# Reciprocal roots of the norms from GpSimd to VectorE, in a hybrid decoder step with expert gathers

## The chip, the cores and the metric

The kernel runs on one core of a Trainium2 chip. The metric is the device time of one execution in microseconds (us). TensorE is called PE (its weight loads PEld), VectorE DVE, ScalarE ACT, GpSimd POOL and SyncE SP.

## The reference, cut to what matters

One layer of a decoder is computed for a prompt of 1024 tokens and for a group of 64 sample tokens (8 sequences of 8), with the same weights.

- `n = RMSNorm(x)`; a wide projection `n @ w_in` feeds three branches: GLA (gated linear attention, with an RMSNorm per head of its output), FoX (softmax attention with forget gates, paged cache for the sample group) and attention over 256 memory tokens, whose keys and values come from `RMSNorm(mem) @ w_mem_kv`.
- `h = x + W_out(sum of gated branches)`.
- `h = h + PEER(RMSNorm(h))`: each token has 8 heads; each head takes the top 16 of 128x128 experts by two lists of keys, and the token's output is a sum over its 128 chosen experts of `gelu(x . u_e) * gate * v_e`.
- `y = RMSNorm(h)`.

`RMSNorm` is `x * rsqrt(mean(x*x) + 1e-6) * g`. All of it is float32. The reciprocal root of one number per row (or two, for the two heads of a GLA half) is all that the change touches in the arithmetic.

## The kernel before, in words

The 1024 prompt tokens are eight blocks (0 to 7) of 128 rows, the sample group is block 8 with 64 rows. `base(grp)` takes three blocks through everything up to the PEER's scores; it runs for `[0, 1, 2]`, `[3, 4, 5]` and `[8, 6, 7]`. In `base` the order of the code is: `norm_T` for the three blocks (load, square sum on ACT, reciprocal root, scaling on DVE, transposes on PE); per half the projections by `mm_w` (raw weights by SP, a rounded high part `wh` on ACT, the rest `wl` on DVE at L267, three matmuls on PE) with `gla` and `fox_prompt` between them; memory attention; the merge; `w_out`; a norm of `h` (`rstd_of`, scaling at L900, transposes at L314); the projection by `w_pq` with the keys' scores (L915) and `top16`.

After that a block goes one of two ways. Blocks 0, 1, 2, 6 and 7 are gathered: `choose(b)` finds the 128 experts of each token, and `peer_gather(b)` fetches, slot by slot, the rows of `peer_u` (L1065) and `peer_v` (L1076) with indirect DMAs that GpSimd issues; DVE multiplies and sums each `u` row tile (L1067) and adds each weighted `v` row tile to `acc` (L1082). The row tiles are four in number (five at the end), so GpSimd's next gather waits until DVE is through with an older row. Blocks 3, 4, 5 and 8 are dense: `expert_weights(b)` spreads the gates over all experts with PE, ACT and DVE, and `peer_dense` multiplies with all 16384 experts on PE at the end. `finish` adds `h`, takes the last norm (L1043 to L1047) and stores a block.

The order of each engine's instructions is written before the run by the framework, from its own estimates and from priorities: `at` gives `choose` and `expert_weights` the most urgent one, `base` the ordinary one by its place in the code, and `gather` a later one, so gathers fill in beside `base` of the next group. Each engine then goes through its own list in order.

The reciprocal roots stand at three places, all on GpSimd: `rstd_of` (called by `norm_T` and for the norm of `h`; L305 and L306), `gla` (L473 and L474, used at L478) and `finish` (L1045 and L1046, used at L1047). Each is two instructions on a tile of one or two columns:

```python
G.tensor_scalar(r, ss, scale, EPS, op0=OP.mult, op1=OP.add)
G.tensor_tensor(r, r, neghalf[:, :n], op=OP.pow)
```

In `gla` the PSUM tile `po`, one of two of the tag `g` that nearly all transposes use, is held until L478 has read it.

Of the kernel before, what the change touches and what calls it, by code (L numbers as in the profile page):

```python
# [18 lines left out]
F32 = mybir.dt.float32  # L19
F32R = mybir.dt.float32r  # L20
BF = mybir.dt.bfloat16
I32 = mybir.dt.int32
# [3 lines left out]
OP = mybir.AluOpType  # L26
AX = mybir.AxisListType

D = 1024
EPS = 1e-6  # L30
# [13 lines left out]
DENSE = [3, 4, 5, SAMPLE]  # L44
# [10 lines left out]
def tile_hybrid(ctx: ExitStack, tc: tile.TileContext, x_prompt, x_sample, cache_fox_k, cache_fox_v,  # L55
# [23 lines left out]
    def T(tag, shape, dt=F32):  # L79
        cnt[0] += 1  # L80
        return bp.tile(shape, dt, tag=tag, name=f"{tag}_{cnt[0]}", bufs=BUFS[tag])

    def const(shape, dt=F32, pool=ec):
        cnt[0] += 1
        return pool.tile(shape, dt, name=f"c{cnt[0]}", tag=f"c{cnt[0]}")
# [128 lines left out]
    pgt = const([64, 1], I32)  # L214
    SP.dma_start(pgt, page_table.rearrange("b (p o) -> (b p) o", o=1))

    neghalf = const([128, 8], F32, cp)
    G.memset(neghalf, -0.5)

    def rows(ap, n, p=128):  # L220

        return bass.AP(tensor=ap.tensor, offset=ap.offset, ap=[[0, p], [1, n]])
# [78 lines left out]

    def rstd_of(ss, n, scale):

        r = T("sm", [128, n])
        G.tensor_scalar(r, ss, scale, EPS, op0=OP.mult, op1=OP.add)  # L305
        G.tensor_tensor(r, r, neghalf[:, :n], op=OP.pow)  # L306
        return r

    def split_T(src_cols, hi, lo, k0):

# [8 lines left out]
    def norm_T(src, nrows, gain, hi, lo):  # L319

        x = T("wr", [128, 1024])
        if nrows < 128:
            G.memset(x, 0.0)
        SP.dma_start(x[:nrows], src)
        ss = T("sm", [128, 1])
        junk = T("P", [128, 1024], BF)
        A.activation(junk, x, AF.Square, accum_out=ss)
        r = rstd_of(ss, 1, 1.0 / D)
        V.scalar_tensor_tensor(x, x, r, gain, op0=OP.mult, op1=OP.mult)
        for k0 in (0, 4):  # L330
            split_T([x[:, (k0 + i) * 128:(k0 + i + 1) * 128] for i in range(4)], hi, lo, k0)
# [57 lines left out]
    def gla(blk, half, qT, zk, zv, zr, glrT, oT):  # L389
        smp = blk == SAMPLE  # L390
        P = 64 if smp else 128
# [77 lines left out]
        junk = T("X", [128, 2, 128])  # L469
        for i in range(2):  # L470
            A.activation(junk[:P, i], po[:P, i * 128:(i + 1) * 128], AF.Square, accum_out=ss[:P, i:i + 1])
        r = T("sm", [128, 2])
        G.tensor_scalar(r[:P], ss[:P], 1.0 / 128, EPS, op0=OP.mult, op1=OP.add)  # L473
        G.tensor_tensor(r[:P], r[:P], neghalf[:P, :2], op=OP.pow)  # L474
        og = T("X", [128, 256])
        for i in range(2):
            sl = slice(i * 128, (i + 1) * 128)
# [160 lines left out]
    def base(grp):  # L638
# [72 lines left out]
        for half in range(2):  # L711
# [9 lines left out]
            if half == 0:  # L721
                px = proj_small()
                glrT = T("sm2", [17, NT])
                G.memset(glrT, 1.0)
                for b in grp:
                    c = T("sm", [128, 16])
                    V.tensor_copy(c, px[b][:, :16])
                    pt = PS("f")
                    PE.transpose(pt[:16, :wid[b]], c[:wid[b]], ident[:wid[b], :wid[b]])
                    evac(glrT[:16, off[b]:off[b] + wid[b]], pt[:16, :wid[b]])  # L730
                    if b == SAMPLE:
                        lfs[0] = logf_sample(px[b][:64, 16:24])
                    else:
                        logf_prompt(b, px[b][:, 16:24])
# [141 lines left out]
        for c in range(4):  # L876
            pz, _ = halves(grp)
            mm_w(w_out[0], 8, c * 256, jobs_of(grp, pz, mT))
            hc = T("z", [128, len(grp), 256])
            for i, b in enumerate(grp):  # L880
                src, n = xsrc(b)
                xc = T("ge", [128, 256])
                if n < 128:
                    G.memset(xc, 0.0)
                SP.dma_start(xc[:n], src[:, c * 256:(c + 1) * 256])
                p = pz[b]
                ht = hc[:, i]
                V.tensor_tensor(ht, p[:, :256], xc, op=OP.add)  # L888
                A.activation(xc, ht, AF.Square, accum_out=ss[b][:, c:c + 1])
                SP.dma_start(h_scr[b][:, c * 256:(c + 1) * 256], ht)  # L890
                h[b].append(ht)
# [146 lines left out]
    def finish(b, y, ht, gfin):  # L1038

        P = 64 if b == SAMPLE else 128  # L1040
        V.tensor_tensor(y[:P], y[:P], ht[:P], op=OP.add)
        s1 = gp.tile([128, 1], F32, tag="fs" if b not in DENSE else "fsd", name=f"fs{b}", bufs=2)
        A.activation(ht[:P], y[:P], AF.Square, accum_out=s1[:P])  # L1043
        r = gp.tile([128, 1], F32, tag="fr" if b not in DENSE else "frd", name=f"fr{b}", bufs=2)
        G.tensor_scalar(r[:P], s1[:P], 1.0 / D, EPS, op0=OP.mult, op1=OP.add)  # L1045
        G.tensor_tensor(r[:P], r[:P], neghalf[:P, :1], op=OP.pow)  # L1046
        V.scalar_tensor_tensor(y[:P], y[:P], r[:P], gfin[:P], op0=OP.mult, op1=OP.mult)  # L1047
        if b == SAMPLE:
            SP.dma_start(y_sample.rearrange("b t d -> (b t) d"), y[:P])
        else:  # L1050
            SP.dma_start(y_prompt[0, b * 128:(b + 1) * 128, :], y)
# [213 lines left out]
    def fox_sample(lfn, oT, fill):  # L1265
# [8 lines left out]
        lf = T("P", [128, 8, 8, 8])  # L1274
        A.activation(lf.rearrange("s b p h -> s h (b p)"), p.rearrange("s (h n) -> s h n", h=8), AF.Copy)
        pre = T("wr", [128, 8, 9, 8])
        G.memset(pre[:, :, 0, :], 0.0)
        for pg in range(8):
            V.tensor_tensor(pre[:, :, pg + 1, :], pre[:, :, pg, :], lf[:, :, pg, :], op=OP.add)
        ndp = []  # L1280
# [12 lines left out]
        evac(ndn, p[:8, :64])  # L1293

        Qz = T("kv", [128, 4, 8, 64])
        G.memset(Qz, 0.0)
        kn = T("zq", [128, 4, 64])
        vn = T("P", [64, 512])
        SP.dma_start(vn, fox_v_sample[0].rearrange("b t h d -> (b t) (h d)"))
# [88 lines left out]

    def mem_sample(qs, oT):
        Qz = T("kv", [128, 4, 8, 32])  # L1390
        G.memset(Qz, 0.0)
        for hh in range(4):
            V.tensor_copy(Qz[:, hh, :, hh * 8:hh * 8 + 8],
                          qs[hh // 2][:, hh % 2, :64].rearrange("p (b t) -> p b t", t=8))
# [126 lines left out]
```

## Time and profile before

| | |
|---|---|
| median of 3 runs | 4340.33 us (4328.08 to 4341.13) |
| profiled execution, its own time | 4325.89 us |
| its span | 4324.1 us |
| busy share of the span | PE 86%, PEld 75%, DVE 77%, ACT 42%, POOL 39% |
| mean granted clock of TensorE | 0.909 of full speed |
| gathers | 640 rows of `u`, 640 of `v` |
| reciprocal roots on POOL | 47 (20 by `rstd_of`, 18 in `gla`, 9 in `finish`) |

Read the span as three stretches. Up to about 650 us `base` of the first group runs without gathers. From there to about 2830 us `base` of the second and third groups share the engines with the gathers of blocks 0, 1 and 2, `choose` and `expert_weights`. From there to the end the dense part runs on PE beside the gathers of blocks 6 and 7.

### The profile page before, as it was taken

The numbers are of one execution on the slowest core, as the hardware profiler recorded it, in microseconds if no ns is written. First come the engines' busy times: TensorE is split into PE (matmuls) and PEld (weight loads), VectorE is DVE, ScalarE is ACT, GpSimd is POOL, SyncE is SP. The second block draws the span as 40 slices with busy tenths as digits, with TensorE's granted clock in tenths as the row PEclk, the third lists the DMA queues.
The fourth block names the chain that finished last, engine by engine and source line by source line (L and its number), as shares of the span: only waits on it lengthen the run. The fifth ranks groups of instructions, "written<-read, shape, count | busy, mean of one in ns | idle before, by whom it ended". The sixth has DMA issues, their size and how long they took to land. (4 is left out here: it accounts for less than half of the span.)

```text
span 4324.1 us, 62414 instructions
## 1 busy us (share of the span) xinstructions
PE 3719.4 (86%) x21306; PEld 3260.5 (75%) x21306; DVE 3338.8 (77%) x7924; ACT 1821.1 (42%) x3710; POOL 1691.6 (39%) x1466
## 2 busy tenths in 40 slices
PE   4999898779777876887888976867999999999997
PEld 4989797768656774776665656756998899889997
DVE  3444479988779898988865458988998888788883
ACT  2565544345444324665664434353332233223322
POOL 0000003554454445446454544414444445454440
PEclk9999998889778976896889998988999999999999
DMA  3334457989889977888888899968989999899992
GB/s 112 109 101 142 138 166 246 307 259 324 282 307 322 307 250 250 285 271 285 286 275 297 282 342 341 321 214 311 310 303 330 338 335 332 315 330 340 342 310 83
DMA packets 665781, 1168.08 MB, mean 270 GB/s; under 512 B 63309, under 2 KB 453093, under 8 KB 661878
## 3 DMA queue, kind: packets, MB, share of 16 engines
q0 software_dynamic: 193616, 704.99, 46.7%
q1 hardware_dynamic: 471846, 459.09, 32.7%
q8 instruction: 169, 2.77, 0.2%
q14 instruction: 150, 1.23, 0.1%
HBM read 1086.82 MB, written 77.11 MB: 269 GB/s over the span
## 5 line engine op out<-in xcount | busy, mean ns | idle before, releaser
L1065 POOL DMA_INDIRECT u<-in_peer_u_dram,ei x640 | 787.2, 1230 | 863.4 <-DVE a L1067 391.2
L1076 POOL DMA_INDIRECT v<-in_peer_v_dram,ei x640 | 764.8, 1195 | 871.5 <-DVE acc L1082 411.7
L1082 DVE SCALAR_TENSOR_TENSOR acc<-v,a,acc 128x1024 f32<-128x1024 f32 x635 | 812.7, 1280 | 68.5 <-DMA v<-in_peer_v_dram,ei 65.5
L1067 DVE CUSTOM_DVE_ANT_0 u<-u,x 128x1024 f32<-128x1024 f32 x640 | 774.4, 1221 | 76.8 <-DMA u<-in_peer_u_dram,ei 76.2
L265 ACT ACTIVATE wh<-wr 128x512 fp32r<-128x512 f32 x568 | 354.3, 630 | 551.8 <-PE pj L274 175.5
L267 DVE TENSOR_TENSOR wl<-wr,wh 128x512 fp32r<-128x512 f32 x568 | 388.7, 688 | 156.7 <-PE pj L277 54.1
L1235 PE MATMUL py<-dwh,dvh 128*128 128x448 f32 x1024 | 375.4, 370 | 35.1 <-ACT dwh L1222 31.0
L1212 PE MATMUL pa<-xh,duh 128*128 128x448 f32 x1024 | 384.5, 375 | 3.9 <-ACT duh L1193 3.9
L273 PE MATMUL pj<-aT,wh 128*128 128x384 f32 (+1 forms) x1104 | 373.6, 344 | 12.1 <-ACT tq L99 7.3
L1213 PE MATMUL pa<-xl,duh 128*128 128x448 f32 x1024 | 380.2, 371 | 0.0
L1236 PE MATMUL py<-dwl,dvh 128*128 128x448 f32 x1024 | 376.0, 368 | 1.5 <-DVE dwl L1223 1.5
L1237 PE MATMUL py<-dwh,dvl 128*128 128x448 f32 x1024 | 374.1, 368 | 2.0 <-DVE dvl L1231 2.0
L274 PE MATMUL pj<-aT,wh 128*128 128x384 f32 (+1 forms) x1104 | 367.9, 337 | 1.5 <-DVE aT L317 1.5
L1230 ACT ACTIVATE dvh<-dvr 128x1024 fp32r<-128x1024 f32 x128 | 134.0, 1058 | 394.1 <-PE py L1236 191.8
L281 PE MATMUL pj<-wh,aT 128*128 128x256 f32 x944 | 263.4, 303 | 36.0 <-DVE z L888 8.8
L282 PE MATMUL pj<-wh,aT 128*128 128x256 f32 x944 | 261.4, 299 | 6.6 <-DVE aT L872 5.3
L277 PE MATMUL pj<-aT,wl 128*128 128x384 f32 (+1 forms) x1104 | 261.6, 341 | 5.8 <-DVE wl L267 5.8
L1215 PE MATMUL pa<-xh,dul 128*128 128x448 f32 x1024 | 239.4, 369 | 0.0
L1235 PEld LDWEIGHTS py<-dwh,dvh 128*128 128x128 f32 x1024 | 192.5, 189 | 52.2 <-ACT dwh L1222 31.2
L273 PEld LDWEIGHTS pj<-aT,wh 128*128 128x128 f32 x1104 | 217.2, 197 | 19.2 <-ACT tq L99 11.4
L281 PEld LDWEIGHTS pj<-wh,aT 128*128 128x128 f32 x944 | 193.4, 206 | 43.0 <-DVE z L739 8.2
L274 PEld LDWEIGHTS pj<-aT,wh 128*128 128x128 f32 x1104 | 217.6, 197 | 2.8 <-DVE aT L317 2.4
(489 smaller groups left out, 8328.5 us busy)
## 6 DMA issues: line engine op xcount, KB each, us to landing
wr<-in_w_in_dram SPq DMA_DIRECT2D x168, 512.0 KB, 5.1
dvr<-in_peer_v_dram SPq DMA_DIRECT2D x128, 512.0 KB, 7.1
dur<-in_peer_u_dram SPq DMA_DIRECT2D x128, 512.0 KB, 6.3
dc<-c_scr SPq DMA_DIRECT2D x15, 1792.0 KB, 16.7
wr<-in_w_pq_dram SPq DMA_DIRECT2D x48, 512.0 KB, 5.7
c_scr<-stg SPq DMA_DIRECT2D x24, 1024.0 KB, 6.3
wr<-in_w_out_dram SPq DMA_DIRECT2D x24, 512.0 KB, 6.4
u<-in_peer_u_dram,ei POOLq DMA_INDIRECT x640, 6.3
```

Source lines behind the costliest of these rows:

```text
L267: V.tensor_tensor(wl, raw[:, q2:q2 + 2], wh.bitcast(F32), op=OP.subtract)
L273: PE.matmul(ps, wh[:, i, c], hi[:, k], start=k == 0, stop=False)
L274: PE.matmul(ps, wh[:, i, c], lo[:, k], start=False, stop=False)
L281: PE.matmul(ps, hi[:, k, :], wh[:, i], start=k == 0 and first, stop=False)
L1065: G.indirect_dma_start(out=r, out_offset=None, in_=UR, in_offset=bass.IndirectOffsetOnAxis(ap=ei[:, s:s + 1], axis=0))
L1067: V.tensor_tensor_reduce(r, r, x2, 1.0, 0.0, OP.mult, OP.add, a[:, s:s + 1])
L1076: G.indirect_dma_start(out=r, out_offset=None, in_=VR, in_offset=bass.IndirectOffsetOnAxis(ap=ei[:, s:s + 1], axis=0))
L1082: V.scalar_tensor_tensor(acc, r, a[:, s:s + 1], acc, op0=OP.mult, op1=OP.add)
L1212: PE.matmul(pa[:, :NT], uh[:, k], xh[:, k], start=k == 0, stop=False)
L1213: PE.matmul(pa[:, :NT], uh[:, k], xl[:, k], start=False, stop=False)
L1235: PE.matmul(py[:, :NT], vh[:, j], wh, start=j == 0, stop=False)
L1236: PE.matmul(py[:, :NT], vh[:, j], wl, start=False, stop=False)
```

## The change: what it does

All 47 reciprocal roots go to VectorE. `rsqrt` makes thirteen instructions of each pair: the scaled sum `x`; its bits as an integer turned into a float, `-0.5 * bits + 1597463007`, turned back into an integer and read as a float, which is a guess `y`; and three Newton steps of three instructions each. Each of the thirteen reads what the one before it wrote. `rstd_of` and `gla` now take three tiles of the tag `sm` (12 buffers) instead of one. The memsets inside the groups (in `norm_T`, `glrT`, the residual's tile, `pre` and the two `Qz`) also go to VectorE; `neghalf` disappears. The memsets of the set-up stay on GpSimd.

```diff
-    neghalf = const([128, 8], F32, cp)
-    G.memset(neghalf, -0.5)
...
     def rstd_of(ss, n, scale):
-        r = T("sm", [128, n])
-        G.tensor_scalar(r, ss, scale, EPS, op0=OP.mult, op1=OP.add)
-        G.tensor_tensor(r, r, neghalf[:, :n], op=OP.pow)
-        return r
+        return rsqrt(ss, scale, [T("sm", [128, n]) for _ in range(3)])
+
+    def rsqrt(ss, scale, tmp):
+        x, y, t = tmp
+        V.tensor_scalar(x, ss, scale, EPS, op0=OP.mult, op1=OP.add)
+        V.tensor_copy(t, x.bitcast(I32))
+        V.tensor_scalar(t, t, -0.5, 1597463007.0, op0=OP.mult, op1=OP.add)
+        V.tensor_copy(y.bitcast(I32), t)
+        for _ in range(3):
+            V.scalar_tensor_tensor(t, y, -0.5, y, op0=OP.mult, op1=OP.mult)
+            V.tensor_tensor(t, t, x, op=OP.mult)
+            V.scalar_tensor_tensor(y, t, 1.5, y, op0=OP.add, op1=OP.mult)
+        return y
...
-            G.memset(x, 0.0)
+            V.memset(x, 0.0)
...
-        r = T("sm", [128, 2])
-        G.tensor_scalar(r[:P], ss[:P], 1.0 / 128, EPS, op0=OP.mult, op1=OP.add)
-        G.tensor_tensor(r[:P], r[:P], neghalf[:P, :2], op=OP.pow)
+        r = rsqrt(ss[:P], 1.0 / 128, [T("sm", [128, 2])[:P] for _ in range(3)])
...
-                G.memset(glrT, 1.0)
+                V.memset(glrT, 1.0)
...
-                    G.memset(xc, 0.0)
+                    V.memset(xc, 0.0)
...
-        r = gp.tile([128, 1], F32, tag="fr" if b not in DENSE else "frd", name=f"fr{b}", bufs=2)
-        G.tensor_scalar(r[:P], s1[:P], 1.0 / D, EPS, op0=OP.mult, op1=OP.add)
-        G.tensor_tensor(r[:P], r[:P], neghalf[:P, :1], op=OP.pow)
+        r = gp.tile([128, 3], F32, tag="fr" if b not in DENSE else "frd", name=f"fr{b}", bufs=2)
+        r = rsqrt(s1[:P], 1.0 / D, [r[:P, i:i + 1] for i in range(3)])
...
-        G.memset(pre[:, :, 0, :], 0.0)
+        V.memset(pre[:, :, 0, :], 0.0)
...
-        G.memset(Qz, 0.0)
+        V.memset(Qz, 0.0)
```

## Rows read from the trace of the kernel before

**Rows 1.** Windows: us; per engine busy us (instructions); granted clock, DMA share, GB/s

```profile
83.00:657.00 574.00, 541.94 (x3593) 504.89 (x3592) 287.63 (x833) 309.95 (x659) 13.51 (x26) 0.96 0.44 132
657.00:1513.00 856.00, 682.60 (x3879) 595.70 (x3879) 737.73 (x1901) 366.42 (x754) 418.10 (x360) 0.84 0.88 296
1513.00:2830.00 1317.00, 1055.39 (x6286) 845.37 (x6286) 1034.45 (x2723) 644.93 (x1455) 634.17 (x535) 0.85 0.85 289
2830.00:4310.00 1480.00, 1409.52 (x7355) 1286.81 (x7355) 1241.84 (x2332) 476.94 (x803) 618.29 (x520) 0.98 0.88 304
```

**Rows 2.** Groups of instructions by line, POOL, 657 to 1513 us

```profile
L1065 POOL DMA_INDIRECT u<-in_peer_u_dram,ei x176 | 216.4, 1229 | 227.0 <-DVE a L1067 89.5 <-DVE acc L1082 32.4 <-DVE tp L933 17.9
L1076 POOL DMA_INDIRECT v<-in_peer_v_dram,ei x156 | 181.3, 1162 | 193.3 <-DVE acc L1082 71.1 <-DMA v<-in_peer_v_dram,ei 15.8 <-DVE a L1067 15.6
```

**Rows 3.** Groups of instructions by line, POOL, whole span

```profile
L474 POOL TENSOR_TENSOR sm<-sm,c 128x2 f32<-128x2 f32 (+1 forms) x18 | 18.3, 1018 | 1.4
L306 POOL TENSOR_TENSOR sm<-sm,c 128x1 f32<-128x1 f32 x20 | 11.6, 585 | 1.4
...
L1046 POOL TENSOR_TENSOR fr<-fr,c 128x1 f32<-128x1 f32 (+1 forms) x9 | 6.3, 699 | 0.6
```

**Rows 4.** Timeline: one reciprocal root of `norm_T` in the first stretch

```profile
50.48 0.19 ACT L327 ACTIVATION_READ_ACCUMULATOR P<-wr 128x1 f32 x1
...
51.64 1.28 DVE L329 SCALAR_TENSOR_TENSOR wr<-wr,sm,kv 128x1024 f32<-128x1024 f32 x1 [0.67 <-POOL sm L306]
```

**Rows 5.** Timeline of DVE, first stretch: L547 needs L545; L727 needs neither

```profile
112.43 0.17 DVE L545 SCALAR_TENSOR_TENSOR sm<-sm,sm 128x8 f32<-128x8 f32 x1
112.63 0.17 DVE L547 TENSOR_TENSOR sm<-sm,sm 128x8 f32<-128x8 f32 x1
112.72 0.17 DVE L727 COPY sm<-f 128x16 f32<-128x16 f32 x1
```

**Rows 6.** Timeline of DVE, second stretch: the same pair, first and last of six

```profile
718.25 0.15 DVE L545 SCALAR_TENSOR_TENSOR sm<-sm,sm 128x8 f32<-128x8 f32 x1
...
722.80 0.24 DVE L547 TENSOR_TENSOR sm<-sm,sm 128x8 f32<-128x8 f32 x1
...
1643.49 0.15 DVE L545 SCALAR_TENSOR_TENSOR sm<-sm,sm 128x8 f32<-128x8 f32 x1
...
1647.69 0.15 DVE L547 TENSOR_TENSOR sm<-sm,sm 128x8 f32<-128x8 f32 x1
```

**Rows 7.** Groups by line, whole span: the `v` half of the gathers' DVE work

```profile
L1082 DVE SCALAR_TENSOR_TENSOR acc<-v,a,acc 128x1024 f32<-128x1024 f32 x635 | 812.7, 1280 | 68.5 <-DMA v<-in_peer_v_dram,ei 65.5
```

**Rows 8.** Timeline: `gla`'s root in the second stretch, first and last of twelve

```profile
809.51 0.20 ACT L471 ACTIVATION_READ_ACCUMULATOR X<-g 128x1 f32 x1
...
815.56 0.60 DVE L478 SCALAR_TENSOR_TENSOR X<-g,sm,z 128x128 f32<-128x128 f32 x2
...
2115.92 0.20 ACT L471 ACTIVATION_READ_ACCUMULATOR X<-g 128x1 f32 x1
...
2120.48 0.61 DVE L478 SCALAR_TENSOR_TENSOR X<-g,sm,z 128x128 f32<-128x128 f32 x2 [1.52 <-POOL sm L474]
```

**Rows 9.** Timeline of PE: first transposes after the norm of `h`, second group

```profile
1425.27 1.12 PE L314 MATMUL g<-c,z 128*128 128x128 f32 x4 [4.29 <-DVE z L900]
```

**Rows 10.** Waits of PE, 657 to 2820 us: us in total, times, longest

```profile
PE g L481 <- DVE X L478: 9.8, 4, 4.6
```

**Rows 11.** Waits of POOL, 657 to 2820 us: us in total, times, longest

```profile
POOL sm L305 <- ACT P L327: 16.9, 5, 5.2
POOL fr L1045 <- ACT h L1043: 3.4, 1, 3.4
```

**Rows 12.** Windows: a slice with many gathers, columns as in the first group

```profile
2376.00:2484.00 108.00, 102.42 (x708) 75.23 (x707) 55.36 (x109) 53.60 (x116) 61.15 (x54) 0.98 0.83 285
```

**Rows 13.** Timeline of DVE: last step of block 7, and of the last block

```profile
4210.28 1.28 DVE L1047 SCALAR_TENSOR_TENSOR acc<-acc,fr,gf 128x1024 f32<-128x1024 f32 x1 [0.74 <-POOL fr L1046]
...
4317.39 1.28 DVE L1047 SCALAR_TENSOR_TENSOR dvr<-dvr,fr,dur 64x1024 f32<-64x1024 f32 x1 [0.97 <-POOL fr L1046]
```

More of the change, by code (lines that the diff above doesn't have):

```diff
@@ L1390, in mem_sample @@
         Qz = T("kv", [128, 4, 8, 32])
-        G.memset(Qz, 0.0)
+        V.memset(Qz, 0.0)
         for hh in range(4):
```

## The prediction, as put on record before the run

> **What bounds the kernel now.** I first cut the span into stretches with the windows view [rows 1]. In the first group (83 to 657 us) PE is busy 542 of 574 us, DVE only half of the time, and there are no gathers. In the dense part (2830 to 4310) PE is busy 1410 of 1480 us at a granted clock of 0.98, so PE sets the length there. Between them nothing is full: DVE is busy 738 of 856 us in the second group and 1034 of 1317 in the third, PE about 80% at a clock near 0.85. The second group has the same prompt work as the first and takes 856 us where that took 574, and the difference is what gathers and `choose` add: 282 us beside 332 gathers [rows 2], 0.85 us a gather. So in the mixed stretch `base` and the gathers lengthen each other although no engine is full.
>
> How they do it shows in the timeline of DVE. A step that needs the step before it starts 0.20 us after it in the first stretch; one that needs nothing follows after 0.09 us [rows 5]. In the mixed stretch the same dependent step starts 4.55 us later in the first pass and 4.20 us in the last of the six [rows 6]: gather sums of 1.28 us [rows 7], `wl` subtractions and top-16 work have been written in between. A chain of small dependent steps on DVE is cheap in busy time there and dear in latency. The change makes 47 such chains (18 in `gla`, 20 in `rstd_of`, 9 in `finish`) [rows 3] of 13 steps.
>
> **The change, part by part.**
>
> *First stretch.* The root on GpSimd now costs 0.97 us from the end of ACT's sum to DVE's use (50.48 + 0.19 to 51.64) [rows 4]. Thirteen dependent steps at 0.20 are 2.6 us, so +1.6 where it stands alone; three blocks interleaved are 39 instructions at 0.09, 3.5 us, +2.5. Three places stand before work that PE has to wait for (memory norms, first norms, the norm of `h`): 7.5 us. Six roots in `gla` at 1.6 are 9.6 if PE has nothing else and 0 if it has; I take half. Sum +12 (between 0 and 17). Here a page speaks: the Trainium skill, "VectorE: DVE Perf Modes", section "The DRAIN you can't avoid", says that a chain of DVE operations takes the same time with a semaphore after each as with one after the last. By it a dependent step would also cost 0.09 us, a lone chain 1.2 us, and this term would be about 8; the trace does not agree (0.20 against 0.09, rows 5), and the row is taken.
>
> *Mixed stretch, latency.* In `gla` a root now takes 5.9 us from ACT's sum to DVE's use at its first pass and 4.4 at its last [rows 8]; I take 5. The new chain's step is bounded by 0.20 us below [rows 5] and by 4.5 above [rows 6]. I take 2.0: where `base` stands still, `wl` work is missing, so a step hosts about one gather sum (1.28) and some top-16 work. 13 x 2.0 = 26, so +21 us per chain. Where does it stand on `base`'s path? At the norm of `h` of both groups PE has nothing else of `base` to do: already now it stands idle 4.29 us there [rows 9]: 2 x 21 = 42. At both groups' first norms the tail of the `w_pq` projection covers some: 2 x 12 = 24. In `gla` (12 times) the next projection covers most; PE waited for L478 four times in this stretch [rows 10], which would make 4/12 x 21 = 7 each, and the order is written knowing the chain: 3 each, 36 (between 0 and 84). Sum 102. But gathers run on while `base` stands: in a slice where they run well GpSimd issues 54 in 108 us, 0.50 a us [rows 12]. 102 us hold 51 gathers, which `base` need not share with later, 0.85 us each: 43 back. Net +59.
>
> *Mixed stretch, GpSimd set free.* GpSimd's queue is in order: a root that waits for ACT parks the gathers behind it. It waited 16.9 + 3.4 = 20 us so between 657 and 2820 [rows 11]; at 332 gathers in 856 us these are 8 gathers, 8 x 0.85 = 7: -7. Nothing larger is to be had: the rest of GpSimd's idle time is waiting for DVE to free a row [rows 2].
>
> *Memsets.* Ten pieces of some 5,900 columns in all; the trace shows no memset on DVE. Bounds: 0 (hidden in its idle time) to 7 us (at the 1.28 us that a sum over 1024 columns takes [rows 7]). +3, between the ends, since some stand in front of a load and some do not.
>
> *Dense part and end.* `finish` of blocks 6 and 7 gets longer, while two row tiles and `acc` are held. Cover: block 7's last step starts at 4210, the end is at 4317 [rows 13], so some 100 us are free: 0. If that cover were gone, 2 x 21 us would be paid. The very last root costs 0.97 us of DVE's wait [rows 13] and becomes 2.6: +2 with the one before it.
>
> Sum: 12 + 59 - 7 + 3 + 2 = +69 us. The profiled execution took 4325.9 us, 14 less than the median of the three runs, so 4395 us; against that median it is +1.3%.
>
> **Rivals.** *A, faster.* The order keeps each chain's steps together (0.20 us, 2.6 us in all), which beats today's 5 us in the mixed stretch. Then the four places there give 4 x 2.4 = 10, `gla` a third of 12 x 2.4, 10, the parked gathers 7, against 6 (half of the first stretch's 12) and 2 at the end: -19, about 4307 us. It decides if a step takes under 5/13 = 0.4 us in the mixed stretch. For it: chains of three blocks can fill each other's gaps. Against it: [rows 6].
>
> *B, DVE's time is all it costs.* The latencies are covered by gathers and projections, and what is left is 27 chains x 13 = 351 instructions at 0.09 us, 32 us, in a stretch where DVE is busy 82% (1772 of 2173 us, rows 1): 26. With +12, -7 and +2 that is +33, 4359 us. The Trainium skill's "Perfetto Trace Analysis", section "Optimizing Scalar/DVE Operations", stands beside this: it advises to take work off a saturated DVE, even to GpSimd, and the change goes the other way. The trace agrees that DVE is the fuller of the two there.
>
> *C, the full latency.* Steps of 3.6 us (47 us, +42 per chain), `gla` a third exposed: 2 x 42 + 2 x 33 + 12 x 14 = 318, 135 given back by gathers: +183 in place of +59, 4519 us. For it: [rows 6], and that `po` holds one of two PSUM tiles `g` through the chain. Against it: gathers that finish early leave DVE to `base`.
>
> **Chances.** The forecast (4355 to 4440) 0.48; B (4335 to 4375) 0.20; C (over 4440) 0.15; A (4290 to 4327) 0.17. About 0.3%, 13 us, is what a measurement of this kernel can tell from no change. From the median 4340 that puts A in faster, 0.17; of B and the forecast's low edge 0.12 within; the rest, 0.71, slower. The likeliest case's own range is 4355 to 4440; the range that holds it 8 times in 10 must reach into A and C: 4310 to 4480, leaving out about 0.1 on each side.
>
> **What would show it.** Right: in the mixed stretch the steps of `rsqrt` start 1.3 to 4 us apart, with L1067, L1082 and L267 between them; PE's wait at the transposes after the norm of `h` grows from 4 to over 15 us; the second and third groups get longer, the dense part (about 1480 us) does not; the first stretch ends some 10 us later. Wrong: steps of 0.2 us everywhere (A); PE's waits at L314 unchanged and only DVE's share up (B). A dense part longer by more than 10 us would say that the end of the gathers has become the bound, which I exclude. The whole order is written anew with the change, so places that it does not touch can move by some us either way.

## The result, and the profile after

The changed kernel takes 4513.2 us (median of 4 runs, 4509.3 to 4517.5) where the kernel before took 4340.7 beside it: a ratio of 1.0417, 95% interval 1.0392 to 1.0442 (the two medians alone give 1.0398). The change makes the kernel slower, as forecast, but by 173 us where 54 were forecast; 4513 lies outside the range (4310 to 4480). Between the two profiled executions it is 183 us against a sum of 69. It is almost the number of rival C, 4519, though not by rival C's terms (below).

First the page's busy times (share of the span, instructions), kernel after:

```profile
span 4507.5 us, 62907 instructions
...
PE 3766.7 (84%) x21306; PEld 3293.6 (73%) x21306; DVE 3408.9 (76%) x8546; ACT 1824.7 (40%) x3710; POOL 1600.4 (36%) x1360
```

Before, the page gave PE 3719.4, DVE 3338.8 and POOL 1691.6 us in a span of 4324.1. The span grows by 183 us, PE's busy time by 47 and DVE's by 70: 136 us of the growth is time in which PE stands still. PE runs the same 21306 matmuls; they took longer, with a mean granted clock of 0.884 where it was 0.909. So the 622 instructions more on DVE are not the bill by themselves; somebody waits for them.

The windows view of the kernel after, cut at the same events as [rows 1] (scaling of the first norms at the start of the first, second and third group, dense part, end):

```profile
87.00:703.00 616.00, 566.58 (x3639) 522.63 (x3637) 330.29 (x1149) 316.65 (x673) 5.72 (x6) 0.92 0.43 129
703.00:1674.00 971.00, 684.38 (x3891) 597.69 (x3891) 825.35 (x2193) 369.25 (x759) 467.25 (x388) 0.81 0.87 291
1674.00:2994.00 1320.00, 1065.12 (x6206) 852.11 (x6206) 962.03 (x2646) 638.35 (x1434) 507.28 (x441) 0.83 0.78 263
2994.00:4494.00 1500.00, 1422.23 (x7361) 1294.57 (x7362) 1246.37 (x2350) 476.87 (x800) 617.20 (x512) 0.97 0.89 299
```

The first window is 42 us longer, the second 115, the third 3, the last 20. The gathers of the second, for [rows 2] (groups by line, POOL, 703 to 1674 us):

```profile
L1070 POOL DMA_INDIRECT u<-in_peer_u_dram,ei x203 | 246.3, 1213 | 260.9 <-DVE a L1072 103.2 <-DVE acc L1087 21.5 <-issue 10.7
L1081 POOL DMA_INDIRECT v<-in_peer_v_dram,ei x185 | 222.8, 1204 | 244.4 <-DVE acc L1087 67.6 <-DVE a L1072 34.9 <-DVE tp L941 14.8
```

388 gathers instead of 332: while `base` stands still in the second group, gathers run on, and the third group has 56 fewer to share with. At the 0.85 us a gather of the prediction these are 48 us, so by that estimate the third window's own losses are some 51 us, not 3.

What a chain looks like. In the first stretch, the timeline of DVE (start, duration, line; the first `gla`; L307 to L310 are the scaled sum and the guess, L312 to L314 a Newton step):

```profile
179.06 0.16 DVE L307 TENSOR_SCALAR sm<-sm 128x2 f32<-128x2 f32 x1
...
181.83 0.16 DVE L312 SCALAR_TENSOR_TENSOR sm<-sm 128x2 f32<-128x2 f32 x1
182.02 0.16 DVE L313 TENSOR_TENSOR sm<-sm,sm 128x2 f32<-128x2 f32 x1
182.22 0.16 DVE L314 SCALAR_TENSOR_TENSOR sm<-sm,sm 128x2 f32<-128x2 f32 x1
```

Steps that depend on each other start 0.20 us apart, as [rows 5] had it, and this chain takes 3.2 us from its first step to its last, one `wl` subtraction included. The Trainium skill ("VectorE: DVE Perf Modes", section "The DRAIN you can't avoid") reports that a chain of copies took the same time with a semaphore after each as with one after the last. No run here compares the two. The prediction drew from it that a dependent step would cost the 0.09 us of an independent one, which is more than the page measured; the trace has 0.20.

In the mixed stretch, the same view for the second `gla` of the second group (for [rows 8]):

```profile
937.49 0.15 DVE L312 SCALAR_TENSOR_TENSOR sm<-sm 128x2 f32<-128x2 f32 x1
937.57 0.21 DVE L1015 SCALAR_TENSOR_TENSOR ch<-ch 128x64 uint32<-128x64 uint32 x1
937.70 1.27 DVE L1087 SCALAR_TENSOR_TENSOR acc<-v,a,acc 128x1024 f32<-128x1024 f32 x1
938.90 0.15 DVE L313 TENSOR_TENSOR sm<-sm,sm 128x2 f32<-128x2 f32 x1
939.28 1.28 DVE L1087 SCALAR_TENSOR_TENSOR acc<-v,a,acc 128x1024 f32<-128x1024 f32 x1 [0.23 <-DMA v<-in_peer_v_dram,ei]
940.48 0.15 DVE L314 SCALAR_TENSOR_TENSOR sm<-sm,sm 128x2 f32<-128x2 f32 x1
941.76 1.28 DVE L1087 SCALAR_TENSOR_TENSOR acc<-v,a,acc 128x1024 f32<-128x1024 f32 x1 [1.13 <-DMA v<-in_peer_v_dram,ei]
942.96 0.15 DVE L312 SCALAR_TENSOR_TENSOR sm<-sm 128x2 f32<-128x2 f32 x1
...
952.22 0.15 DVE L314 SCALAR_TENSOR_TENSOR sm<-sm,sm 128x2 f32<-128x2 f32 x1
953.10 1.28 DVE L1087 SCALAR_TENSOR_TENSOR acc<-v,a,acc 128x1024 f32<-128x1024 f32 x1 [0.74 <-DMA v<-in_peer_v_dram,ei]
954.31 0.60 DVE L484 SCALAR_TENSOR_TENSOR X<-g,sm,z 128x128 f32<-128x128 f32 x2
```

Between any two steps stands one gather sum of 1.28 us, and some of these wait up to 1.21 us (one of the lines left out) for their row's transfer, with the next step, which is ready, parked behind them. That is where 2 us a step come from. This chain takes 23.7 us from its first step to its last (928.51 to 952.22); the twelve of `gla` in the mixed stretch take 4.9 to 32.9, and 23.7 in the mean. And PE meanwhile (timeline of PE):

```profile
924.36 1.06 PE L467 MATMUL g<-z,kE 128*128 128x128 f32 x4
954.71 0.73 PE L487 MATMUL g<-c,X 128*128 128x128 f32 x2 [29.29 <-DVE X L484]
955.37 1.22 PE L403 MATMUL g<-c,sm 17*128 17x256 f32 x2
```

PE does nothing for 29 us, then the transposes, and right behind them L403, the first matmul of the next block's `gla`. The cover that the prediction counted on was used up. Of the projections that follow `gla` in the code, the two in row form (L278 to L282) ended at 829 and the third was evicted at 841; the gate projections (L270 to L274) covered the chain of the half's first block (848 to 872) and ended at 883:

```profile
829.23 0.64 PE L282 MATMUL pj<-wl,aT 128*128 128x256 f32 x4
...
882.43 0.86 PE L274 MATMUL pj<-aT,wl 128*128 128x384 f32 x4
```

PE's waits from the norm of `h` of the first group on (570 to 2830 us: total, times, longest), for [rows 10]:

```profile
PE g L487 <- DVE X L484: 55.2, 5, 29.3
PE f L921 <- ACT zt L99: 40.8, 9, 9.9
...
PE g L322 <- DVE wr L337: 20.1, 4, 11.8
```

The wait at `gla`'s transposes goes from 9.8 to 55.2 us, in five of the twelve places; at the other seven PE had other work ahead of them. The other two rows stand at the first norms: their transposes (L322), and the keys' scores beside them (L921), which wait until older scores are evicted. Before the change they were 3.5 and 3.4 us.

The wait behind the norm of `h`, where the prediction had put its largest certain term, hardly grew. For [rows 9], the first transposes of the second and third groups (timeline of PE):

```profile
1527.66 1.54 PE L322 MATMUL g<-c,z 128*128 128x128 f32 x6 [6.16 <-DVE sm L312]
...
2905.02 1.94 PE L322 MATMUL g<-c,z 128*128 128x128 f32 x8 [4.76 <-DVE z L906]
```

Before these waits were 4.29 and 4.55 us. From the last matmul ahead of the norm to the first one of the projection behind it PE took 20.3 and 12.7 us, where it took 16.9 and 17.5.

The three `gla` of a half follow each other. From the first one's L403 to the last one's transposes, the windows view gives for the kernel before:

```profile
755.00:931.00 176.00, 121.60 (x745) 108.50 (x743) 162.36 (x507) 62.27 (x120) 93.97 (x80) 0.79 0.87 289
1021.00:1159.00 138.00, 116.34 (x705) 104.53 (x704) 110.57 (x215) 64.92 (x122) 66.81 (x60) 0.89 0.90 310
1649.00:1839.00 190.00, 134.87 (x768) 113.26 (x769) 176.02 (x565) 100.95 (x234) 93.98 (x74) 0.72 0.81 269
1953.00:2121.00 168.00, 135.25 (x764) 114.46 (x764) 140.14 (x297) 98.92 (x229) 94.65 (x71) 0.76 0.85 295
```

and for the kernel after:

```profile
793.00:1036.00 243.00, 142.62 (x910) 127.55 (x908) 213.12 (x580) 76.52 (x145) 133.39 (x108) 0.78 0.87 290
1115.00:1278.00 163.00, 122.00 (x713) 106.83 (x711) 134.54 (x276) 71.04 (x132) 83.83 (x66) 0.82 0.91 308
1774.00:2047.00 273.00, 196.18 (x1103) 163.90 (x1100) 249.54 (x829) 152.83 (x365) 114.35 (x91) 0.72 0.81 267
2124.00:2345.00 221.00, 171.89 (x876) 139.75 (x875) 179.02 (x424) 133.22 (x311) 85.20 (x78) 0.72 0.80 270
```

Together 900 us instead of 672, +228. PE's work in them is 633 us instead of 508 (3602 matmuls instead of 2982), so 125 of the 228 hold work that has moved in from elsewhere, and PE's idle time grows by 103 (164 to 267). The two places of the first norms in the mixed stretch (norm of `h` to the last transposes of L322) show the same on a smaller scale, for the kernel after:

```profile
597.00:736.00 139.00, 102.65 (x577) 98.53 (x577) 126.41 (x640) 45.67 (x93) 19.12 (x20) 0.78 0.54 166
1527.00:1701.00 174.00, 114.03 (x569) 103.41 (x570) 165.19 (x637) 45.70 (x93) 63.44 (x57) 0.74 0.79 251
```

Before they took 102 and 121 us with PE busy 91.8 and 94.8: +90 us, of them 60 idle.

The end, for [rows 13] (timeline of DVE, the last root): eight dependent steps at 0.18 us in an empty queue, then the use.

```profile
4500.64 0.14 DVE L313 TENSOR_TENSOR fr<-fr 64x1 f32<-64x1 f32 x1
...
4501.93 0.15 DVE L314 SCALAR_TENSOR_TENSOR fr<-fr 64x1 f32<-64x1 f32 x1
4502.12 1.28 DVE L1052 SCALAR_TENSOR_TENSOR dvr<-dvr,fr,dur 64x1024 f32<-64x1024 f32 x1
```

### The profile page after: what moved, and what is told of

Its sections match the earlier page's. It is cut to its first block, busy times and chain, and to the rows that moved or that the text cites. A ratio compares the mean times of both kernels' runs of the same rounds, so it can differ in the third digit from the quotient of the medians.

```text
span 4507.5 us, 62907 instructions
## 1 busy us (share of the span) xinstructions
PE 3766.7 (84%) x21306; PEld 3293.6 (73%) x21306; DVE 3408.9 (76%) x8546; ACT 1824.7 (40%) x3710; POOL 1600.4 (36%) x1360
## 4 chain that ended last, share of the span: by engine, by line
PE 28%; issue 10%; DMA 6%; DVE 4%; POOL 2%; ACT 2%; SPq 0%; POOLq 0%; ACTq 0%; DVEq 0%
PE pa L1220 4%; PE pa L1217 4%; PE pa L1218 3%; PE py L1240 3%; PE py L1241 3%; PE py L1242 3%; DMA dvr<-in_peer_v_dram 3%; PE pt L1196 2%; DMA v<-in_peer_v_dram,ei 1%; DVE u L1072 1%; PE cw L1147 1%; POOL v L1081 1%; POOL u L1070 1%; DVE acc L1087 1%; PE f L1336 1%
## 5 line engine op out<-in xcount | busy, mean ns | idle before, releaser
L1070 POOL DMA_INDIRECT u<-in_peer_u_dram,ei x640 | 770.5, 1204 | 1778.8 <-DVE tp L941 699.9
L1081 POOL DMA_INDIRECT v<-in_peer_v_dram,ei x640 | 753.9, 1178 | 917.4 <-DVE acc L1087 379.1
L264 DVE TENSOR_TENSOR wl<-wr,wh 128x512 fp32r<-128x512 f32 x568 | 386.6, 684 | 170.8 <-PE pj L274 51.2
L270 PE MATMUL pj<-aT,wh 128*128 128x384 f32 (+1 forms) x1104 | 373.5, 343 | 7.4 <-ACT tq L99 4.4
L274 PE MATMUL pj<-aT,wl 128*128 128x384 f32 (+1 forms) x1104 | 263.1, 342 | 14.8 <-DVE wl L264 14.7
L278 PE MATMUL pj<-wh,aT 128*128 128x256 f32 x944 | 257.8, 297 | 20.4 <-DVE z L745 8.0
L1147 PE MATMUL cw<-hot,hot 128*128 128x128 f32 x768 | 175.4, 366 | 111.9 <-ACT stg L1148 82.7
L279 PE MATMUL pj<-wh,aT 128*128 128x256 f32 x944 | 255.5, 294 | 5.5 <-DVE aT L878 5.3
L1147 PEld LDWEIGHTS cw<-hot,hot 128*128 128x128 f32 x768 | 137.8, 252 | 155.2 <-ACT stg L1148 115.0
L270 PEld LDWEIGHTS pj<-aT,wh 128*128 128x128 f32 x1104 | 217.0, 197 | 14.9 <-ACT tq L99 8.4
```

The lines of the kernel that those rows point to most:

```text
L264: V.tensor_tensor(wl, raw[:, q2:q2 + 2], wh.bitcast(F32), op=OP.subtract)
L270: PE.matmul(ps, wh[:, i, c], hi[:, k], start=k == 0, stop=False)
L1070: G.indirect_dma_start(out=r, out_offset=None, in_=UR, in_offset=bass.IndirectOffsetOnAxis(ap=ei[:, s:s + 1], axis=0))
L1081: G.indirect_dma_start(out=r, out_offset=None, in_=VR, in_offset=bass.IndirectOffsetOnAxis(ap=ei[:, s:s + 1], axis=0))
```

## The experiments

Every run is given as its median and its ratio to the kernel before on the same chip, with the 95% interval. The change itself stands at 1.0417.

### Which place pays

**Roots back on GpSimd, one place at a time** (the changed kernel, everything else as changed).

```diff
+    def pool_rsqrt(ss, scale, r, n):
+        G.tensor_scalar(r, ss, scale, EPS, op0=OP.mult, op1=OP.add)
+        G.tensor_tensor(r, r, neghalf[:r.shape[0], :n], op=OP.pow)
+        return r
...
-        r = rsqrt(ss[:P], 1.0 / 128, [T("sm", [128, 2])[:P] for _ in range(3)])
+        r = pool_rsqrt(ss[:P], 1.0 / 128, T("sm", [128, 2])[:P], 2)
```

The first norms (`norm_T`) alone:

> The changed kernel, with the roots of norm_T alone (11 of 47) back on GpSimd. Latency theory (the 13 steps of a chain are stretched by work written in between, and base waits for the chain): the two group starts give back what the changed trace shows there, 37 and 53 us, so about 4420 us (4400 to 4440). Engine-time theory (DVE's extra instructions are the cost): 143 fewer instructions at 0.09 us are 13 us, so about 4500. Order theory (any change of the written order moves the time by such amounts): no relation, anywhere from 4340 to 4520.

`gla` alone, as in the diff:

> The changed kernel, with gla's 18 roots back on GpSimd. Latency theory: the bodies of the second and third groups got 47 and 23 us longer, mostly by these, so about 4440 us (4420 to 4470). Engine-time theory: 234 instructions at 0.09 us, 21 us, so about 4492. Order theory: no relation.

Both:

> The changed kernel with the roots of norm_T and of gla back on GpSimd; only the norm of h, the last norm and the memsets stay on DVE. Latency theory, parts adding up: 4513 - 136 - 24 = 4353 us (4340 to 4370). Order theory: no relation to the parts.

| back on GpSimd | us | ratio |
|---|---|---|
| first norms | 4489.1 | 1.0340 (1.0321 to 1.0358) |
| `gla` | 4377.2 | 1.0086 (1.0057 to 1.0115) |
| both | 4347.1 | 1.0054 (1.0032 to 1.0076) |

The first norms give back 24 us by the medians (0.8 points of the ratio), a quarter of what was expected: the wait at their transposes is gone, but the one at `gla`'s grows from 55.2 to 72.1 us. `gla` gives back 136 us (3.3 points) and is the main place; the wait at its transposes falls to 12.6 us. What is left with both undone is half a percent: the norm of `h`, `finish` and the memsets together.

**Only `gla`'s roots on VectorE** (the kernel before with that one part of the change).

```diff
-        r = T("sm", [128, 2])
-        G.tensor_scalar(r[:P], ss[:P], 1.0 / 128, EPS, op0=OP.mult, op1=OP.add)
-        G.tensor_tensor(r[:P], r[:P], neghalf[:P, :2], op=OP.pow)
+        r = rsqrt(ss[:P], 1.0 / 128, [T("sm", [128, 2])[:P] for _ in range(3)])
```

> The kernel before with gla's 18 roots alone as chains of 13 steps on DVE; everything else as before. Latency theory, parts adding up: 4340 + 136 = 4476 us (4440 to 4490). Engine-time theory: 234 instructions at 0.09 us, 21 us, so 4361. Order theory: no relation.

4442.0 us, ratio 1.0260 (1.0215 to 1.0305): 18 of the 47 roots cost most of it from the other side too, with PE waiting 63.6 us at the transposes. It is inside the expected range, 34 us below its middle figure.

### Latency or DVE's time

**One Newton step, and six** in place of three (7 and 22 steps a chain; the first leaves out two of the three refinements of the root).

```diff
-        for _ in range(3):
+        for _ in range(1):
```

> The changed kernel with one Newton step in place of three: 7 instructions in a chain instead of 13. It leaves out two of the three refinements, so the roots are only good to about 0.2 per cent. Latency theory: with today's 5 us of the old path worth about 2 steps, the excess of 172 us shrinks to 5/11, 78 us, so about 4419 us (4395 to 4445). Engine-time theory: 282 fewer instructions at 0.09 us, 25 us, so about 4488. Order theory: no relation to the number of steps.

> The changed kernel with six Newton steps in place of three: 22 instructions in a chain (the extra three change nothing in the result). Latency theory: by 7 steps at 4425 and 13 at 4513, 14.7 us a step, so 4645 us (4600 to 4690). Engine-time theory: 423 instructions at 0.09 us, 38 us, so 4551.

4424.7 us, ratio 1.0210 (1.0177 to 1.0244), and 4651.8 us, 1.0743 (1.0710 to 1.0776): both as expected. Per step of the chain that is 0.0207 / 6 = 0.0035 and 0.0326 / 9 = 0.0036 of 4330, 15 us a step over the whole range. At 2 us a step, that is as much as seven or eight chains with their full length on the path, or six if the 3.4 us that a step costs when nobody waits for it (44 us for 13 steps, the next experiment) are taken off first.

**The same chains, unused** (the kernel before with its roots on GpSimd, and beside each one the 13 steps on VectorE into tiles that nobody reads).

```diff
         G.tensor_tensor(r, r, neghalf[:, :n], op=OP.pow)
+        rsqrt(ss, scale, [T("dd", [128, n]) for _ in range(3)])
         return r
```

> The kernel before, with all its roots still on GpSimd, and beside each of the 47 the chain of 13 steps on DVE into tiles that nobody reads. Engine-time theory: the same 611 DVE instructions as in the change, so most of its 172 us: about 4500. Latency theory: nobody waits for these chains, so only their busy time and their room in DVE's queue: 4345 to 4375.

4369.8 us, ratio 1.0101 (1.0077 to 1.0126). The same 611 instructions cost 44 us when nobody waits for them, so of 4.2% one is DVE's time and its places in the queue, and 3.2 are left, by subtraction, for the waiting. That is rival B's mechanism at about its size (33 us), and it is a quarter of the whole.

**The steps first in rank** (the changed kernel; each chain gets the most urgent priority when the order is written).

```diff
+        keep, tc.cur_priority = tc.cur_priority, 0
...
+        tc.cur_priority = keep
```

> The changed kernel, with the 13 instructions of each root given the most urgent priority of all. If the steps are late because other work is ranked before them, they now follow each other closely (0.2 to 0.5 us) and the time falls to 4380 us or less. If they are late because in the written order a dependent step is not ready when the one before it is issued, so that something else is taken at each step, they stay 1.3 to 3 us apart and the time at 4480 to 4520. Engine-time theory: 4513, nothing changes.

4503.9 us, ratio 1.0361 (1.0317 to 1.0405), PE's wait at the transposes 59.1 us: almost nothing. `gla`'s twelve chains in the mixed stretch take 23.3 us in the mean, as before the edit. That fits the second theory, in which a step's successor is not ready yet when the order is written and a gather sum that is takes the place; what the framework saw as ready is not on record. Either way rival A, steps kept together, is not to be had by rank.

**Root on ScalarE** (three steps instead of thirteen).

```diff
-        for _ in range(3):
...
+        A.activation(t, x, AF.Sqrt)
+        V.reciprocal(y, t)
```

> The changed kernel, with the guess and the Newton steps replaced by a square root on ScalarE and a reciprocal on DVE: a chain of three steps, GpSimd still free of roots. Latency theory: with three steps of about 2 us nearly all the excess goes, and what GpSimd's freedom is worth shows: 4330 to 4365 us, plus what ScalarE's table changes cost if it must load the square root's table each time (1.28 us a load, up to 94 loads, not all on the path). Engine-time theory: 10 x 47 fewer instructions at 0.09 us, 42 us, so about 4471.

4370.7 us, ratio 1.0101 (1.0052 to 1.0149). Shorter, and still not the kernel before. The groups of ACT by line show one price, a table load at 29 of the 47 roots; with the loads that other functions now need again, ACT has 182 of them in place of the changed kernel's 135, 60 us more:

```profile
L308 ACT ACT_TABLE_LOAD x29 | 37.2, 1283 | 0.5
```

### What hands `gla`'s delay on

Five suspects were tried: the PSUM tile that is held, the place of the transposes in the code, SP's queue, the projection behind, and the next `gla`.

**The output copied to SBUF** (the changed kernel; frees `po` before the chain).

```diff
+        pc = T("pc", [128, 256])
+        evac(pc[:P], po[:P, :256])
+        po = pc
```

> The changed kernel, with gla's output copied by ScalarE from PSUM to SBUF (256 columns, 18 times) before the root, so that the PSUM tile po is free during the chain. If the held PSUM tile is what makes gla's chains dear, most of gla's 136 us come back: 4390 to 4430 us. If PE waits for the scaled output itself at its transposes, which stand next in its queue, nothing changes: 4500 to 4530.

4518.7 us, ratio 1.0441 (1.0396 to 1.0486): no gain, PE's wait 64.2 us. The held tile, which the prediction named under rival C, is not it.

**The tail later in the code** (scaling, transposes, eviction and store are called behind the next projection), on both kernels.

```diff
             proj(C_FK + half * 256, fin_k)
+            rest()
             for b in grp[1:2]:
-                branch1(b)
+                rest = branch1(b)
```

> The changed kernel, with what follows the root in gla (scaling, transposes, store) put behind the projection that comes after gla in the code, so that PE meets these transposes in its queue later. If PE's wait at these transposes, which stand next in its queue, is the cost of gla's chains, most of their 136 us come back: 4380 to 4430. If the chains are dear by something else (DVE's order, the tiles they hold), it stays above 4480.

> The kernel before with the same move of gla's tail. PE waits only 10 us for that scaling in the mixed stretch, so at most that: 4325 to 4345 us; if the PSUM tile held longer stands in the way, up to 4400.

4504.9 us, ratio 1.0398 (1.0358 to 1.0438), and 4327.7 us, 1.0009 (0.9992 to 1.0027). The first says nothing about its theory: PE still meets the transposes straight ahead of the next `gla`, at 879 and 956 us, and waits 54.4 us for them.

**The store from ACT's queue.** SP stood still at `gla`'s store for 158.3 us in the mixed stretch of the changed kernel (7 times, longest 60.3), in front of weight loads.

```diff
-            SP.dma_start(o_scr[b][:, br, 2 * half:2 * half + 2, :wid[b]], t[:, :, :wid[b]])
+            (SP if br else A).dma_start(o_scr[b][:, br, 2 * half:2 * half + 2, :wid[b]], t[:, :, :wid[b]])
```

> The changed kernel with the stores of gla's results issued from ACT's queue, behind the eviction that they need, in place of SP's. Theory S (SP is parked at that store during a chain, 158 us in all in the mixed stretch, and the next weights are loaded late because of it): most of gla's 136 us come back, 4380 to 4430 us. Theory P (PE itself is parked at gla's transposes, which stand in its list ahead of the next gla and projection): weights that come earlier help little, 4480 to 4520 us.

> The kernel before with the same store issued from ACT's queue. Theory S: SP waited 89 us at this store in the mixed stretch of the kernel before, in part ahead of weights: 4300 to 4325 us, faster than both. Theory P: no change, 4325 to 4355 us.

4528.7 us, ratio 1.0476 (1.0456 to 1.0496), and on the kernel before 4329.5 us, 0.9995 (0.9978 to 1.0011). SP's wait at this store is gone from the trace and nothing comes back; part of it stands elsewhere in SP's queue, where the wait of the weight loads for L264 goes from 367.5 to 457.3 us (745 to 2900). A long wait in a queue is not a cost by itself.

**The transposes held behind the projection** by data: `og` gets a tile of its own, and one small instruction adds zero times a result of the next projection.

```diff
+        def tail(mark):
+            V.scalar_tensor_tensor(og[:P, :1], mark[:P], 0.0, og[:P, :1], op0=OP.mult, op1=OP.add)
...
             proj(C_FV + half * 256, fin_v)
+            rest(vv[:, grp[-1], :1])
```

> The changed kernel with gla's scaled output in a tile of its own, and one more small instruction on it that adds zero times a result of the next projection, so that the transposes, their eviction and the store can't stand ahead of that projection in any list. Theory P (PE parked at the transposes): the waits there go from 55 to under 15 us and the time falls to 4400 to 4460 us. Theory D (what counts is that DVE itself is slowed, so that gla's other steps and the projections' evictions come late whatever PE does): 4480 to 4530 us.

> The kernel before with the transposes held behind the next projection. Theory P: PE waited 9.8 us there, so 4325 to 4345 us, no change; it is the control for the same edit on the changed kernel. Theory D: the same, no change. A time above 4360 would say that holding the transposes costs something by itself (a tile held longer, a small instruction more), which must then be added to the other run's reading.

4530.8 us, ratio 1.0484 (1.0466 to 1.0503), and 4331.0 us, 1.0014 (0.9999 to 1.0029). Again no gain, and PE's waits show why:

```profile
PE g L489 <- DVE og L486: 68.8, 7, 26.8
```

The projections named in the edit had run long before (in the kernel after by 841, the second block's transposes at 954), so "behind the projection" changed nothing. What stands behind the transposes in PE's list is the next `gla` (L403 above).

**The next `gla` first.** The output is copied as above, and a block's transposes are held by data until the next block's `gla` has its scores, so that the next head runs beside the chain.

```diff
+        if prev:
+            prev(att[:, 0, :1])
         ex = X[:, :, 1]
...
-        og = T("X", [128, 256])
+        og = pc
...
+        def tail(mark=None):
+            if mark is not None:
+                V.scalar_tensor_tensor(og[:P, :1], mark[:P], 0.0, og[:P, :1], op0=OP.mult, op1=OP.add)
...
-                branch1(b)
+                rest = branch1(b, rest)
```

> The changed kernel with gla's output copied out of PSUM and a block's transposes, eviction and store held until the next block's gla has come to its scores (one small instruction more, which adds zero times a column of them), so that in PE's list the next gla's head stands directly behind the last matmul of this one and the transposes behind that head. Theory G (the three gla of a half follow one another, each head written behind the transposes of the one before, and in the mixed stretch no projection is left to fill the gap, so a chain of 20 to 30 us adds itself to the path): the chains run beside the next head, PE's waits at the transposes go from 55 to under 20 us, and 60 to 110 of gla's 136 us come back: 4400 to 4455 us. Theory D (DVE's list is what is late, so the head, which takes a dozen turns on DVE and ACT itself, is only slowed by as much as the chain gains): 4490 to 4530 us.

> The kernel before with the same edit. Theory G: the root and the transposes that leave the path are only some 7 us long at 12 places, less the copy and the added instruction: 4270 to 4320 us, faster than both. Theory D: 4325 to 4360 us.

On the changed kernel 4456.0 us, ratio 1.0282 (1.0250 to 1.0314): 57 us back, 1 us above the expected range. On the kernel before 4297.4 us, ratio 0.9921 (0.9897 to 0.9944): 0.8% faster than the kernel before, clear of the noise. The windows of the first, cut as above:

```profile
774.00:973.00 199.00, 141.74 (x926) 126.70 (x927) 183.36 (x558) 74.60 (x146) 103.95 (x82) 0.83 0.88 292
1052.00:1207.00 155.00, 121.46 (x713) 106.32 (x711) 128.95 (x272) 73.70 (x135) 71.93 (x60) 0.85 0.89 305
1691.00:1946.00 255.00, 187.94 (x1070) 156.95 (x1069) 227.32 (x748) 141.24 (x327) 120.17 (x85) 0.75 0.79 262
2026.00:2207.00 181.00, 146.58 (x793) 119.15 (x791) 146.90 (x373) 107.63 (x250) 76.78 (x59) 0.75 0.82 275
```

790 us instead of 900, and PE's idle time in them is 192 instead of 267, most of the way back to 164. The wait at the transposes is 28.7 us in two rows, where under 20 was expected:

```profile
PE g L495 <- DVE pc L489: 18.4, 2, 9.8
...
PE g L495 <- DVE pc L492: 10.3, 5, 6.2
```

The theory holds in its place but not in its full size. Part of the 57 us is a gain that the kernel before has too (36), so the chains' own share is about 21, a sixth of `gla`'s 136. The next head is no free cover: it takes turns on DVE and ACT itself, and in this kernel PE waited 16.9 us once inside a head (L410 for ACT's L406). So what hands on the greater part of the 136 us is not shown: the held tile, SP's queue and the projection behind are cleared, and the next `gla` carries a part. Between this kernel and its twin on GpSimd there are still 159 us; how they split between heads slowed by the chains, the last `gla` of each half (no head follows it), the first norms and the rest was not measured.

## Why the prediction was right in direction and wrong in size

- **The step.** 2.0 us was taken between 0.20 and 4.5, and the chains in `gla` measure it: each gap between two steps from 931 to 952 us holds one gather sum, and the twelve chains take 23.7 us in the mean. The forecast of 26 us a chain stands there, though not everywhere: at the first norms a chain takes 26 to 39 us in the second group and 40 to 47 in the third, at the norm of `h` 2 to 11. C came to the right number by luck: its 3.6 us a step holds at most at the first norms, and its 84 us at the norm of `h` did not come.
- **`gla`: the step that failed.** "In `gla` (12 times) the next projection covers most" and "3 each, 36 (between 0 and 84)". Measured: 136 us come back when `gla` alone is undone, 11 a place over twelve. Its term in the sum, less the share given back by gathers and with the half of 9.6 us from the first stretch, was about 26, so this step alone is some 110 us of the 114 by which the profiled executions missed the sum (183 for 69). In place, PE's idle time grew by 103 us over the twelve. The prediction read cover from PE's waits before [rows 10]: 4 waits of 12, 9.8 us. But a wait that is short for a root of 5 us tells only that 5 us were covered, not that 26 would be. What was ahead in PE's list should have been read: the projections and gates had run by 883, the second block's transposes were at 954, and the next thing was the next `gla`, which stood behind them. That the cover failed is shown by undoing `gla`; that the next `gla` behind the transposes is the way is shown for about 21 us, and for the rest the cause stays open.
- **Norm of `h`, 2 x 21: too large.** Its chains took 14 and 8.5 us from first to last step for three blocks, and PE's wait behind it went from 4.29 to 6.16 and from 4.55 to 4.76 us, where over 15 was the sign of being right. Three chains side by side fill each other's gaps there, as rival A had it.
- **First norms, 2 x 12: too small in place, about right in the total.** The three chains took 57 and 69 us, and the two places grew by 90 us, 30 of them PE work; undoing them returned 24.
- **Given back by gathers, 43 of 102: about right, the reason open.** 56 more gathers ran in the second group, 48 us by the prediction's price. Along PE's list from the norm of `h` of the first group to the dense part, the stretch as a whole grew by 145 us (2268 to 2413) with the same matmuls, and PE's idle time by 122 (445 to 567). In the places of the first norms and of `gla` it grew by 163, so 41 us of idle time went away elsewhere, which is about the forecast; that gathers are the reason is not shown. The gathers of blocks 0 to 2 ended at 2804, and the last 206 us before the dense part had none.
- **First stretch, +12 (0 to 17):** the norm of `h` came 19 us later (578 to 597), a little above the bound; the rest of the first window's 42 us lies at the second group's first norms.
- **GpSimd set free, -7; memsets, +3; end, +2.** None can be seen by itself. The roots' waits of [rows 11] are gone from POOL. The memsets took 0.9 to 1.8 us on DVE for a large tile; the three, with `finish` and the norm of `h`, make the 0.5% that is left when both other places are undone.
- **Dense part.** It was to stay within 10 us and took 21 more (1471 to 1492 between its first matmul and the last use of a root). PE's own work there is 13 us longer at a granted clock of 0.97 where it was 0.98. The gathers of blocks 0 to 2 are not the reason: they ended 200 us ahead of it, and the dense part had its own 512. Other orders moved this part too (1452 in the faster kernel, 1510 with the next `gla` first, 1463 with `gla`'s roots back on GpSimd, 1458 with only those on VectorE), so it stays open whether the chains have to do with it.
- **Rival B** is refuted as the whole (1.0101 against 1.0417) and confirmed as a part. **Rival A** is refuted: 0.20 us holds in the first stretch; in the mixed stretch two of `gla`'s twelve chains come near it (4.9 and 7.6 us), but the mean is 23.7.

The Trainium skill's "Perfetto Trace Analysis", section "Optimizing Scalar/DVE Operations", says that it may make sense to take work off a saturated DVE, even to GpSimd, though between these two it might not help. Here taking the roots of both norms back to GpSimd helped (1.0417 to 1.0054), but by latency more than by load: DVE's busy share is 77% before the change and 76% after it.

## What to carry to other kernels

A lone chain of n dependent instructions on a shared engine costs n times whatever stands between two steps, here 2 us for 0.16 us of work; before moving a short dependent calculation, count its steps and look at what its new neighbours are. Here two slow instructions on a quiet engine beat thirteen fast ones on a busy one. Cover has to be read as work: find what the waiting engine has next in its list and whether that is ready, since the length of today's wait bounds nothing for a longer delay. And when a wait is found that could be the carrier, take it away before believing in it: SP's 158 us at one store gave nothing back, and the next `gla` first gave back less than it seemed to, since the kernel before gained too.

## What the runs showed of the hardware that was not expected

- `Sqrt` on ScalarE brought a table load of 1283 ns in 29 of 47 cases, 37 us, and more loads at other functions: 47 more in all, one for each root.
- With chains interleaved and nothing else in the queue, steps of different chains start 0.07 to 0.12 us apart (598.46, 598.53, 598.65, 598.73 us), where dependent ones start 0.18 to 0.20 apart. At the norm of `h` of the first group three chains take 7.1 us with two scalings and a subtraction among them (594.33 to 601.45); the quickest single chain took 2.3 (2901.85 to 2904.19).
